# The down projection of a feed-forward block by Strassen's products, with right operands kept in DRAM

## The chip, the cores and the metric

The kernel runs on one core of a Trainium2 chip. The metric is device time in microseconds of one execution; the profile shows one such execution instruction by instruction. All times of the trace are counted from its first instruction.

## The reference, cut to what matters

One decoder block over 1024 tokens of 1024 features, in float32: an mLSTM and a pooling branch, merged by gates, then a gated feed-forward part with 2816 hidden features, and a last norm.

```python
x = x + (g_a * y_a + g_b * y_b) @ w_out[l]
h2 = rms_norm(x, norm2_g[l])
x = x + (silu(h2 @ w_ffn_gate[l]) * (h2 @ w_ffn_up[l])) @ w_ffn_down[l]
return rms_norm(x, final_norm_g)
```

The change is in the product with `w_ffn_down`, (1024 x 2816) @ (2816 x 1024), in what comes before and after it, and in one scratch tile of the mLSTM.

## The kernel before

Tokens lie along the free dimension and features on the 128 partitions, so a tile is 128 features by 1024 tokens, cut into two halves of 512 tokens. There are 8 feature tiles (`KT`) and 22 hidden tiles (`NFF`). Every float32 operand is split into a rounded part and a remainder (`split`, L126 to L128: a cast on ScalarE, a subtraction on VectorE), and `mm3` (L137 to L141) makes a product of two split operands by three matmuls in fp32r.

The stages follow each other: values and gates of the mLSTM, the input projection, the mLSTM itself, the two branches, the output projection, gate/up, down. The input projection and gate/up are done by Strassen's products in Winograd's form (`products`, L209 on): two output tiles at a time, their 8 contraction tiles taken as 4 pairs, in seven products of 4 x 3 matmuls in place of eight. Results are summed from three banks of PSUM, A, B and C, by copies on ScalarE (L219, L221, L223) and sums on VectorE (L225, L227, L229). `pipeline` makes the left operands of job n + 1 ahead of the products of job n. In gate/up a job is one hidden tile: gate and up of that tile are its two outputs. `gated` (L824 on) multiplies by the norm, applies silu (L838 to L841) and stores the hidden tile into `g_d` in DRAM. The right operands of gate/up (`T`, seven kinds by four pairs, x times the norm's gain) stay in SBUF for all 22 jobs.

Down is done without Strassen's products. For the first 512 tokens the loop runs over the hidden tiles outside and the 8 feature tiles inside, with eight banks of PSUM open at once: it loads `w_down[k]` and half of `g_d[k]`, splits both (`first`, `hidden`), and splits the other half of the tile into `gT` for later. Then the norm over these 512 tokens is made and the results are scaled and stored (L908, L909) while the second half runs: feature tile by feature tile, over all 22 hidden tiles, with `w_downc`, the same weights in another order. The last feature tile is done in two pieces of 256 tokens, and the results of the second half are turned by TensorE and stored by rows.

The program is traced by Tile. A planner puts the instructions of each engine in order by its own estimate of the times; where the text has `issue_after`, an instruction is held behind another one of the same engine. Loads and most stores go through the queue of SyncE (SP), in order. Pools reuse memory tile by tile: a tile of a later pool waits for the last reader of the tile that lay there.

In the mLSTM's `attend`, `hf` (two tiles) first takes the squares of the normed numerator (L665, only their sum is used) and then the scaled numerator (L675) that TensorE turns (L677).

Of the kernel before, what the change touches and what calls it, by code (L numbers as in the profile page):

```python
# [8 lines left out]
F32 = mybir.dt.float32  # L9
F32R = mybir.dt.float32r  # L10
# [34 lines left out]
EARLY = 2  # L45
# [18 lines left out]
def tile_hybrid_block(ctx, tc, x, xt, consts, params, w_fm, w_v, w_pool, w_a, w_b, w_out, w_gate, w_up, w_down, w_downc, out, out_rows):  # L64
# [42 lines left out]
    g_d = dram.tile([NFF, P, S], F32, name="g_d")  # L107
# [52 lines left out]
    def operand(dst, src):  # L160
        split(dst[:, 0, :], dst[:, 1, :], src)

    def first_difference(T, kp, lo_k):

        b11, b12 = halves(lo_k)
        nc.vector.tensor_sub(out=b11, in0=b12, in1=b11)
        operand(T["d1"][kp], b11)

    def other_operands(T, kp, lo_k, hi_k, plain=True):

        (b11, b12), (b21, b22) = halves(lo_k), halves(hi_k)
        nc.vector.tensor_sub(out=b11, in0=b22, in1=b11)
        yield operand(T["d2"][kp], b11)
        if plain:
            yield operand(T["b21"][kp], b21)
        nc.vector.tensor_sub(out=b12, in0=b22, in1=b12)
        yield operand(T["d3"][kp], b12)
        if plain:
            yield operand(T["b22"][kp], b22)
        nc.vector.tensor_sub(out=b21, in0=b11, in1=b21)  # L180
        yield operand(T["d4"][kp], b21)
# [167 lines left out]
    with tc.issue_after(stored):  # L349
        for kp in range(KH):  # L350
            first_difference(T, kp, xg[kp])
            list(other_operands(T, kp, xg[kp], xg[kp + KH], False))
# [193 lines left out]
    with ExitStack() as c4:  # L546
# [91 lines left out]
        def attend(h, c, it, state):  # L638
# [3 lines left out]
            nums, hfs = [], []  # L642
            for jj in range(2):
# [20 lines left out]
                hfs.append(t2.tile([P, DH], F32, tag="hf", name="hf"))  # L664
                nc.scalar.activation(out=hfs[jj], in_=num[:, :DH], func=AF.Square, scale=r, accum_out=ss[:, jj:jj + 1])  # L665
# [7 lines left out]
            for jj in range(2):  # L673
                hf = hfs[jj]
# [91 lines left out]
    with ExitStack() as c5:  # L766
# [4 lines left out]
        sq = pool(c9, "sqp", 1, "right").tile([P, S], F32, name="sq")  # L771
        sps = [sp0, None, None]
        ffn = [(w_gate[j], w_up[j]) for j in range(NFF)]
        with ExitStack() as c6:
            xp = pool(c6, "xp", 3, "right")
            pending = None
            for n, j in enumerate(a + b for a in range(KH) for b in (0, KH)):
# [17 lines left out]
                if j < KH:  # L795
                    pending = xs
                    operand(T["b11"][j], halves(xs)[0])
                    first_difference(T, j, xs)
# [4 lines left out]
                list(other_operands(T, j - KH, pending, xs))  # L803
            c3.close()
            sps[1] = pool(c5, "sf1", 6)
# [7 lines left out]
            made = other_operands(T, KH - 1, pending, xs)  # L813
# [6 lines left out]
        ev = pool(c5, "evf", 8)  # L820
        ws.extend(later)
        made_last = split.last

        def gated(j, outs, u1):  # L824
# [8 lines left out]
            for n, (z, u, r) in enumerate(((z2, u2, rsb2[1]), (z1, u1, rsb2[0]))):  # L833
                with ExitStack() as order:
                    if j == NFF - 1 and n >= 0:
                        for made in first.made:
                            order.enter_context(tc.issue_after(made))
# [4 lines left out]
            nc.sync.dma_start(out=g_d[j], in_=outs[0])  # L842
# [14 lines left out]
        dp = pool(c7, "dp", 6, "right")  # L857
        gp = pool(c7, "gp", 6, "right")

        def hidden(pl, k, half):  # L860
            t = pl.tile([P, 2, 512], F32R, tag="g", name="g")
            operand(t, load(g_d[k, :, half * 512:(half + 1) * 512], 512))
            return t

        def first(k):
            w = parts(dp, "d", load(w_down[k]), "wd"), hidden(gp, k, 0)
            if k == 0:
                first.made = split.last
            return w

        ready = [first(k) for k in range(EARLY)]
        last()
    x3p = pool(c7, "x3p", KT, "right")
    sm = pool(c7, "smd", 2, "right")
    gp1 = pool(c7, "gp1", NFF)
    op = pool(c7, "op", 4)

    def residual(j, half, ps):
        r = x3p.tile([P, 512], F32, tag="x3", name="x3")
        with tc.issue_after(load.last.ins):  # L880
            nc.sync.dma_start(out=r, in_=x2_d[j, :, half * 512:(half + 1) * 512])
        nc.vector.tensor_add(out=r, in0=ps, in1=r)
        return r

    def square(r):
        sq = sm.tile([P, 512], F32, tag="sq", name="sq")
        nc.scalar.activation(out=sq, in_=r, func=AF.Square)
        return sq


    ps = [bank("mm" if j < 6 else "aux") for j in range(KT)]
    gT = []
    for k in range(NFF):
        w, g = ready.pop(0) if ready else first(k)
        gT.append(hidden(gp1, k, 1))
        for j in range(KT):
            mm3(ps[j], [a[:, j * P:(j + 1) * P] for a in w], [g[:, a, :] for a in range(2)], k == 0, k == NFF - 1)
    x3 = [residual(j, 0, ps[j]) for j in range(KT)]
    acc = square(x3[0])
    for r in x3[1:]:  # L900
        sq = square(r)
        nc.vector.tensor_add(out=sq, in0=acc, in1=sq)
        acc = sq
    rs = sm.tile([P, 4], F32, tag="rs", name="rs3")
    inverse_rms(sm, token_sums(acc, 4), rs)
    along_rows(sm, rsb2[0], rs, gp.tile([P, 2, 512], F32R, tag="g", name="diag"), 4)
    for j, r in enumerate(x3):
        nc.vector.scalar_tensor_tensor(out=r, in0=r, scalar=col(A_NF, j), in1=rsb2[0], op0=ALU.mult, op1=ALU.mult)  # L908
        nc.sync.dma_start(out=out[j], in_=r)  # L909


    x3 = []
    rows = [op.tile([P, D], F32, tag="o", name="o") for _ in range(4)]
    LAST = KT - 1

# [9 lines left out]
    def feature(j, w, ps, sl, k0, n):  # L925
        for i in range(n):
            k = k0 + i
            mm3(ps, [a[:, i * P:(i + 1) * P] for a in w], [gT[k][:, a, sl] for a in range(2)], k == 0, k == NFF - 1)

    def down_weights(j, k0):  # L930
        n = min(8, NFF - k0)
        return parts(dp, "d", load(w_downc[j, :, k0 * P:(k0 + n) * P], n * P), "wd"), k0, n

    chunks = range(0, NFF, 8)
    for j in range(LAST):
        ps = bank()
        for k0 in chunks:
            w, k0, n = down_weights(j, k0)
            feature(j, w, ps, slice(0, 512), k0, n)
        r = residual(j, 1, ps)  # L940
        sq = square(r)
        nc.scalar.activation(out=r, in_=r, func=AF.Copy, scale=col(A_NF, j))
        x3.append(r)
        if j > 0:
            nc.vector.tensor_add(out=sq, in0=acc, in1=sq)
        acc = sq
        if j == 4:
            for t in range(4):
                turn(t, 0, 4)
    ws = [down_weights(LAST, k0) for k0 in chunks]  # L950
    r = x3p.tile([P, 512], F32, tag="x3", name="x3")
    with tc.issue_after(load.last.ins):
        nc.sync.dma_start(out=r, in_=x2_d[LAST, :, 512:1024])
    x3.append(r)
    sq = sm.tile([P, 512], F32, tag="sq", name="sq")
    ms = sm.tile([P, 4], F32, tag="ms", name="ms")
    rs = sm.tile([P, 4], F32, tag="rs", name="rs3")
    for p in range(2):
# [3 lines left out]
        for w, k0, n in ws:  # L962
            feature(LAST, w, ps, sl, k0, n)
            if p == 0 and k0 == 0:
                for t in range(4):
                    turn(t, 4, LAST)
                nc.vector.tensor_scalar(out=ms, in0=token_sums(acc, 4), scalar1=1.0 / D, scalar2=EPS, op0=ALU.mult, op1=ALU.add)
# [79 lines left out]
```

## Time and profile before

| what | us |
|---|---|
| median of 3 runs (1522.51 to 1526.81) | 1524.85 |
| the profiled execution, whole | 1523.66 |
| its span, first to last instruction | 1521.9 |
| TensorE busy (7237 matmuls) | 1505.1 |
| weight loads busy | 1270.2 |
| VectorE busy | 1018.5 |
| ScalarE busy | 708.9 |

A matmul's end is modelled, and one begins before the one ahead of it has ended, so its work is read from the distance of starts and from the waits, and not from the busy time alone.

### The profile page before, as it was taken

How to read it: one execution, taken by the hardware profiler on the slowest of the kernel's cores; microseconds unless marked ns; L12 is line 12 of the kernel's file. 1: busy time of each engine (PE TensorE's matmuls, PEld its weight loads, DVE VectorE, ACT ScalarE, POOL GpSimd, SP SyncE). 2: the span in 40 equal slices, each digit the busy share in tenths (PEclk: the TensorE clock that was granted, in tenths of full speed). 3: DMA queues.
4: the chain of work that ended last, by engine and by line, in shares of the span. 5: the costliest groups of instructions: out<-in, count | busy, mean ns of one | idle time of the engine just before them, and what ended most of it. 6: DMA issues, size and time to landing. Idle time of an engine off the chain costs nothing.

```text
span 1521.9 us, 19329 instructions
## 1 busy us (share of the span) xinstructions
PE 1505.1 (99%) x7237; PEld 1270.2 (83%) x7237; DVE 1018.5 (67%) x1801; ACT 708.9 (47%) x1256; POOL 27.8 (2%) x58
## 2 busy tenths in 40 slices
PE   9999999999999999999999999999999999999998
PEld 9998888878887799988888788888888888888887
DVE  6767878788867677757567776666666655554432
ACT  6475655566543578752133453333333324443332
POOL 0000000000000011100000000000000000000000
PEclk9999999999999999999999999999999999999999
DMA  6663333323323697718334322222222224664531
GB/s 216 217 230 109 138 120 127 118 105 125 131 84 118 241 324 253 226 57 324 111 131 140 103 83 79 83 83 83 83 83 83 83 77 161 225 220 158 180 107 56
DMA packets 92942, 216.04 MB, mean 142 GB/s; under 512 B 8876, under 2 KB 44844, under 8 KB 92848
## 3 DMA queue, kind: packets, MB, share of 16 engines
q1 hardware_dynamic: 77680, 174.95, 34.6%
q10 hardware_dynamic: 15168, 39.85, 6.9%
q8 instruction: 57, 0.93, 0.3%
q14 instruction: 37, 0.30, 0.1%
HBM read 154.98 MB, written 59.79 MB: 141 GB/s over the span
## 4 chain that ended last, share of the span: by engine, by line
PE 95%; DMA 1%; DVE 1%; ACT 1%; issue 1%; SPq 0%; POOL 0%; POOLq 0%; ACTq 0%; DVEq 0%
PE mm L139 26%; PE mm L141 26%; PE mm L140 26%; PE mm L151 14%; PE aux L141 1%; PE aux L139 1%; PE aux L140 1%; DMA raw<-in_w_a 1%; PE mm L517 0%; PE aux L677 0%; DMA z_d<-o 0%; DMA o<-in_xt 0%; PE aux L566 0%; PE aux L273 0%; DMA rc<-z_d 0%
## 5 line engine op out<-in xcount | busy, mean ns | idle before, releaser
L127 ACT CAST s<-raw 128x512 fp32r<-128x512 f32 x220 | 131.9, 620 | 150.0 <-PE mm L141 106.5
L128 DVE TENSOR_TENSOR s<-raw,s 128x512 fp32r<-128x512 f32 x220 | 147.4, 687 | 36.8 <-ACT s L127 36.3
L139 PE MATMUL mm<-zd,s 128*128 128x512 f32 x352 | 137.5, 393 | 0.3 <-DVE o L227 0.3
L140 PE MATMUL mm<-fd,s 128*128 128x512 f32 x352 | 137.7, 391 | 0.0
L139 PE MATMUL mm<-fd,s 128*128 128x512 f32 x352 | 134.7, 392 | 2.6 <-ACT e L219 2.2
L141 PE MATMUL mm<-fd,s 128*128 128x512 f32 x352 | 137.3, 390 | 0.0
L141 PE MATMUL mm<-zd,s 128*128 128x512 f32 x352 | 137.3, 390 | 0.0
L140 PE MATMUL mm<-zd,s 128*128 128x512 f32 x352 | 137.1, 389 | 0.0
L141 PE MATMUL mm<-g,wdl 128*128 128x512 f32 (+1 forms) x330 | 123.3, 376 | 0.0
L140 PE MATMUL mm<-g,wdh 128*128 128x512 f32 (+1 forms) x330 | 123.1, 375 | 0.0
L139 PE MATMUL mm<-g,wdh 128*128 128x512 f32 (+1 forms) x330 | 120.5, 375 | 0.0
L139 PE MATMUL mm<-zb,s 128*128 128x512 f32 x264 | 103.9, 394 | 0.0
L839 ACT ACTIVATE e<-e 128x512 f32<-128x512 f32 x44 | 27.8, 633 | 162.0 <-DVE e L838 162.0
L128 DVE TENSOR_TENSOR wdl<-raw,wdh 128x1024 fp32r<-128x1024 f32 (+1 forms) x46 | 54.1, 1177 | 73.0 <-ACT wdh L127 73.0
L141 PE MATMUL mm<-fb,s 128*128 128x512 f32 x264 | 102.8, 389 | 0.0
L140 PE MATMUL mm<-zb,s 128*128 128x512 f32 x264 | 102.8, 389 | 0.0
L141 PE MATMUL mm<-zb,s 128*128 128x512 f32 x264 | 102.7, 390 | 0.0
L140 PE MATMUL mm<-fb,s 128*128 128x512 f32 x264 | 102.7, 389 | 0.0
L139 PE MATMUL mm<-fb,s 128*128 128x512 f32 x264 | 99.8, 389 | 0.0
L127 ACT CAST wdh<-raw 128x1024 fp32r<-128x1024 f32 (+1 forms) x46 | 46.7, 1014 | 91.8 <-PE mm L140 54.0
L139 PEld LDWEIGHTS mm<-fd,s 128*128 128x128 f32 x352 | 66.4, 189 | 17.5 <-ACT e L219 2.9
L139 PEld LDWEIGHTS mm<-zd,s 128*128 128x128 f32 x352 | 66.1, 188 | 14.8 <-DVE o L227 0.8
(323 smaller groups left out, 3432.7 us busy)
## 6 DMA issues: line engine op xcount, KB each, us to landing
raw<-in_w_fm SPq DMA_DIRECT2D x44, 512.0 KB, 3.7
z_d<-o ACTq DMA_DIRECT2D x24, 512.0 KB, 2.9
raw<-in_w_gate SPq DMA_DIRECT2D x22, 512.0 KB, 3.7
raw<-in_w_up SPq DMA_DIRECT2D x22, 512.0 KB, 4.2
g_d<-e SPq DMA_DIRECT2D x22, 512.0 KB, 2.6
raw<-in_w_down SPq DMA_DIRECT2D x22, 512.0 KB, 4.3
raw<-g_d SPq DMA_DIRECT2D x44, 256.0 KB, 3.4
q_d<-x ACTq DMA_DIRECT2D x16, 512.0 KB, 2.7
```

The source lines that it names most:

```text
L127: hi_made = nc.scalar.copy(out=hi, in_=src)
L128: split.last = hi_made.ins, nc.vector.tensor_sub(out=lo, in0=src, in1=hi.bitcast(F32)).ins
L139: nc.tensor.matmul(out, lhsT=l[0], rhs=r[0], start=start, stop=False, skip_group_check=resume)
L140: nc.tensor.matmul(out, lhsT=l[0], rhs=r[1], start=False, stop=False, skip_group_check=resume)
L141: mm3.last = nc.tensor.matmul(out, lhsT=l[1], rhs=r[0], start=False, stop=stop, skip_group_check=resume)
L151: nc.tensor.matmul(ps[half], lhsT=l[a], rhs=r[half][b], start=(k == 0 and (a, b) == (0, 0)), stop=(k == nk - 1 and a == 1),)
L839: nc.scalar.activation(out=z, in_=z, func=AF.Silu)
```

## The change

The down projection is done by Strassen's products too, in Winograd's form, for all 1024 tokens at once. The 22 hidden tiles are taken as 11 pairs. The seven right operands of each pair are made as the hidden tiles come out of gate/up: `hidden` splits each into a staging tile (`stage`, three tiles that rotate) and stores it, hi and lo, in `tg_d` in DRAM; of each pair, b11 and d1 are made after the even job, d2, b21 and d3 after the odd one, b22 and d4 after the next even one. `g_d` is gone, and so is one of the two copies of the weights.

The down stage runs over three chunks of 4, 3 and 4 pairs; in a chunk over the seven products (`STEPS`); in a product over the four pairs of feature tiles. The right operands of a step are loaded while the step before runs (13 tiles), left operands are made four products ahead (`EARLY`, 6 tiles), and weights for the next chunk are loaded in the third and the sixth step. After each product VectorE adds the bank to x, which lies in SBUF as 8 tiles for all tokens. In the last chunk the squares are summed as the tiles become final. The two halves of tokens change places: the first 512 are now written by rows at the end, the last 512 by columns.

The pools `sf1` and `evf` have one tile less each, to make room. In the mLSTM the squares go into `rsb`, which is free there, and `hf` is taken only for the scaled values.

```diff
-EARLY = 2
+NPAIR = NFF // 2
+CHUNKS = ((0, 4), (4, 7), (7, 11))
+EARLY = 4
...
-    g_d = dram.tile([NFF, P, S], F32, name="g_d")
+    tg_d = dram.tile([NPAIR, 7, P, S], F32, name="tg_d")
...
-                hfs.append(t2.tile([P, DH], F32, tag="hf", name="hf"))
-                nc.scalar.activation(out=hfs[jj], in_=num[:, :DH], func=AF.Square, scale=r, accum_out=ss[:, jj:jj + 1])
+                nc.scalar.activation(out=rsb[:, jj * DH:(jj + 1) * DH], in_=num[:, :DH], func=AF.Square, scale=r, accum_out=ss[:, jj:jj + 1])
...
-                hf = hfs[jj]
+                hf = t2.tile([P, DH], F32, tag="hf", name="hf")
...
-            sps[1] = pool(c5, "sf1", 6)
+            sps[1] = pool(c5, "sf1", 5)
...
-        ev = pool(c5, "evf", 8)
+        ev = pool(c5, "evf", 7)
+        stp = pool(c5, "stp", 2)
...
+        places = [sqp, stp, stp]
+        def stage(i, b, src):
+            t = places[len(staged) % len(places)].tile([P, 2, 512], F32R, tag="t", name="t")
+            staged.append(t)
+            operand(t, src)
+            nc.sync.dma_start(out=tg_d[i, OPS.index(b)].rearrange("p (a n) -> p a n", a=2), in_=t.bitcast(F32))
+        def hidden(j, z):
+            put = partial(stage, j // 2)
+            if j % 2 == 0:
+                if rest:
+                    list(rest.pop())
+                put("b11", halves(z)[0])
+                first_difference(put, z)
+                even.append(z)
+            else:
+                made = other_operands(put, even.pop(), z)
+                for _ in range(3):
+                    next(made)
+                rest.append(made)
...
-            nc.sync.dma_start(out=g_d[j], in_=outs[0])
+            hidden(j, outs[0])
...
+        s1p = pool(c7, "s1p", KH, "right")
+        rbp = pool(c7, "rbp", KH, "right")
+        tgp = pool(c7, "tgp", 13, "right")
+        ap = pool(c7, "ap", 6, "right")
+        STEPS = ("b21", "d1", "b22", "b11", "d2", "d3", "d4")
+        def down_weights(c, q, fh):
+            k0, k1 = CHUNKS[c]
+            t = (rbp if fh else rawp).tile([P, S], F32, tag="rb" if fh else "raw", name="rb" if fh else "raw")
+            n = (k1 - k0) * P
+            nc.sync.dma_start(out=t[:, :2 * n], in_=w_down[q, fh, :, 2 * k0 * P:2 * k1 * P])
+        def down_lefts(c, q):
...
+            yield op(a12)
...
+            nc.vector.tensor_add(out=s1, in0=a21, in1=a22)
+            t = op(s1)
+            nc.vector.tensor_sub(out=a21, in0=a11, in1=a21)
+            nc.vector.tensor_sub(out=s1, in0=s1, in1=a11)
+            nc.vector.tensor_sub(out=a12, in0=a12, in1=s1)
+            yield t
+            yield op(a12)
+            yield op(a11)
+            yield op(s1)
+            yield op(a21)
+            nc.scalar.activation(out=t[:, 0, :], in_=a22, func=AF.Copy, scale=-1.0)
+            nc.vector.scalar_tensor_tensor(out=t[:, 1, :], in0=a22, scalar=-1.0, in1=t[:, 0, :].bitcast(F32), op0=ALU.mult, op1=ALU.subtract)
+            yield t
+        def down_rights(c, s):
+            for i in range(*CHUNKS[c]):
+                t = tgp.tile([P, 2, 512], F32R, tag="tg", name="tg")
+                nc.sync.dma_start(out=t.bitcast(F32), in_=tg_d[i, OPS.index(STEPS[s])].rearrange("p (a n) -> p a n", a=2))
+        for q in range(KH):
+            down_weights(0, q, 0)
+        down_rights(0, 0)
+        for q in range(KH):
+            down_weights(0, q, 1)
+        for e in range(EARLY):
+            make_ready(e)
         last()
+        list(rest.pop())
...
+    for j in range(KT):
+        t = x3p.tile([P, S], F32, tag="x3", name="x3")
+        nc.sync.dma_start(out=t, in_=x2_d[j])
...
+    def later_tokens():
+        rs = sm.tile([P, 4], F32, tag="rs", name="rs3")
+        inverse_rms(sm, token_sums(acc[1], 4), rs)
+        along_rows(sm, rsb2[0], rs, ap.tile([P, 2, 512], F32R, tag="a", name="diag"), 4)
+        for j in range(KT):
+            r = halves(x3[j])[1]
+            nc.vector.scalar_tensor_tensor(out=r, in0=r, scalar=col(A_NF, j), in1=rsb2[0], op0=ALU.mult, op1=ALU.mult)
+            nc.sync.dma_start(out=out[j], in_=r)
...
+    for e, (c, s, q) in enumerate(entries):
+        final = c == len(CHUNKS) - 1
+        if q == 0:
+            if s + 1 < len(STEPS):
+                down_rights(c, s + 1)
+            elif not final:
+                down_rights(c + 1, 0)
+        make_ready(e + EARLY)
+        if s == 2 and not final:
+            down_weights(c + 1, q, 0)
+        if s == 5 and not final:
+            down_weights(c + 1, q, 1)
+        a, ts = todo.pop(0), rights[c, s]
+        if final and s == 6 and q == KH - 1:
+            break
+        if s == 0:
+            ps = bank()
+        elif s in (1, 2):
+            ps = C[q] = bank() if s == 1 else C[q]
+        else:
+            ps = A[q] = bank() if s == 3 else A[q]
+        product(ps, a, ts, whole, s in (0, 1, 3), True)
+        o = (o10, o21, o11, o10, o11, o21, o20)[s]
+        nc.vector.tensor_add(out=o, in0=ps, in1=o)
...
+        if s == 5:
+            square(q + KH, 1)
+            if q == KH - 1:
+                nc.vector.tensor_add(out=o20, in0=ps, in1=o20)
+                later_tokens()
...
+        product(ps, left, right, sl, True, True)
```

The last product of the last chunk is done in two pieces of 256 tokens, as the last feature tile was before, with the 12 turns of feature tiles 4 to 6 behind the first piece.

## Rows read from the trace of the kernel before

**Rows 1.** The page: span, and busy us of the engines.
```profile
span 1521.9 us, 19329 instructions
...
PE 1505.1 (99%) x7237; PEld 1270.2 (83%) x7237; DVE 1018.5 (67%) x1801; ACT 708.9 (47%) x1256; POOL 27.8 (2%) x58
```

**Rows 2.** The page: the chain that ended last, by engine.
```profile
PE 95%; DMA 1%; DVE 1%; ACT 1%; issue 1%; SPq 0%; POOL 0%; POOLq 0%; ACTq 0%; DVEq 0%
```

**Rows 3.** Stretches: us, busy PE, PEld, DVE, ACT, POOL (instructions); clock, DMA share, GB/s.
```profile
890.00:1250.00 360.00, 360.00 (x1590) 298.09 (x1589) 243.26 (x379) 129.00 (x228) 0.00 (x0) 1.00 0.24 84
260.00:400.00 140.00, 140.00 (x633) 113.53 (x632) 116.76 (x199) 83.75 (x114) 0.00 (x0) 1.00 0.37 128
...
1267.00:1387.00 120.00, 120.00 (x532) 99.34 (x531) 63.11 (x78) 50.25 (x68) 0.00 (x0) 1.00 0.68 226
1387.00:1514.00 127.00, 126.70 (x647) 108.26 (x645) 48.91 (x67) 40.75 (x60) 1.71 (x2) 1.00 0.34 107
```

**Rows 4.** TensorE's waits over the whole run: us in total, times, longest.
```profile
PE mm L139 <- ACT e L219: 2.2, 1, 2.2
...
PE mm L151 <- ACT ya L127: 0.5, 1, 0.5
...
PE mm L139 <- DVE e L227: 0.4, 1, 0.4
```

**Rows 5.** Groups by form, TensorE, 1260 to 1522: busy us, mean ns, idle before.
```profile
L139 PE MATMUL mm<-g,wdh 128*128 128x512 f32 x286 | 107.9, 389 | 0.0
...
L139 PE MATMUL aux<-g,wdh 128*128 128x512 f32 x44 | 16.5, 389 | 0.0
...
L139 PE MATMUL mm<-g,wdh 128*128 128x256 f32 x44 | 12.5, 285 | 0.0
```

**Rows 6.** Timeline, full matmuls of the down stage: start us, us, instruction.
```profile
1359.79 0.39 PE L139 MATMUL mm<-g,wdh 128*128 128x512 f32 x1
...
1370.67 0.39 PE L139 MATMUL mm<-g,wdh 128*128 128x512 f32 x1
```

**Rows 7.** Timeline, half matmuls of the last feature tile.
```profile
1509.47 0.28 PE L141 MATMUL mm<-g,wdl 128*128 128x256 f32 x1
...
1513.43 0.28 PE L141 MATMUL mm<-g,wdl 128*128 128x256 f32 x1
```

**Rows 8.** Timeline, VectorE in gate/up; in brackets the idle time before.
```profile
1119.60 0.69 DVE L202 TENSOR_TENSOR raw<-raw 128x512 f32<-128x512 f32 x1
1120.20 0.68 DVE L841 TENSOR_TENSOR e<-mm,e 128x512 f32<-128x512 f32 x1
...
1127.50 0.69 DVE L840 TENSOR_TENSOR e<-e,rsb 128x512 f32<-128x512 f32 x1 [0.70 <-ACT e L839]
...
1139.24 0.68 DVE L841 TENSOR_TENSOR e<-mm,e 128x512 f32<-128x512 f32 x1
```

**Rows 9.** Groups: ScalarE's cast (whole run), VectorE's half (890 to 1250).
```profile
L127 ACT CAST s<-raw 128x512 fp32r<-128x512 f32 x220 | 131.9, 620 | 150.0 <-PE mm L141 106.5 <-DVE raw L197 29.9 <-PE mm L151 4.8
...
L128 DVE TENSOR_TENSOR s<-raw,s 128x512 fp32r<-128x512 f32 x91 | 59.8, 689 | 19.4 <-ACT s L127 19.4
```

**Rows 10.** DMA issues: KB each, median us from issue to landing.
```profile
g_d<-e SPq DMA_DIRECT2D x22, 512.0 KB, 2.6
```

**Rows 11.** Stretches with the busiest DMA on rows of 4 KB.
```profile
690.00:700.00 10.00, 10.00 (x46) 8.29 (x45) 9.35 (x13) 2.84 (x5) 0.00 (x0) 1.00 0.98 379
700.00:710.00 10.00, 10.00 (x46) 8.29 (x45) 8.22 (x12) 2.74 (x4) 0.00 (x0) 1.00 0.98 338
```

**Rows 12.** Timeline, VectorE, the norm of the first 512 tokens.
```profile
1406.11 0.16 DVE L253 TENSOR_SCALAR ms<-aux 128x4 f32<-128x4 f32 x1 [2.31 <-PE aux L273]
...
1416.22 5.38 DVE L908 SCALAR_TENSOR_TENSOR x<-x,par,rsb 128x512 f32<-128x512 f32 x8
```

**Rows 13.** The stretch around TensorE's wait at the entry of gate/up.
```profile
850.00:855.00 5.00, 2.76 (x9) 1.91 (x8) 4.84 (x8) 2.20 (x5) 0.00 (x0) 0.82 0.28 82
```

**Rows 14.** ScalarE's waits in the mLSTM, 540 to 690.
```profile
ACT hf L665 <- PE aux L677: 6.3, 3, 4.4
```

More of the change, by code (lines that the diff above doesn't have):

```diff
@@ L856, in tile_hybrid_block @@
         c7 = ctx.enter_context(ExitStack())
[L857 to L869, printed above, removed]
@@ L872, in tile_hybrid_block @@
+        early_made = []
+        for q in range(KH):
[5 more added lines that the diff above has]
+            make_ready(e)
+            if e == 1:
+                early_made.extend(split.last)
         last()
-    x3p = pool(c7, "x3p", KT, "right")
-    sm = pool(c7, "smd", 2, "right")
-    gp1 = pool(c7, "gp1", NFF)
+        list(rest.pop())
+    x3p = pool(c7, "x3p", KT)
     op = pool(c7, "op", 4)
[L878 to L909, printed above, removed]
+    sm = pool(c7, "smd", 2)
@@ L916, in turn, with scaled @@
+    def scaled(j):
+        r = halves(x3[j])[0]
+        nc.scalar.activation(out=r, in_=r, func=AF.Copy, scale=col(A_NF, j))
     def turn(t, j0, j1):
@@ L923, in turn @@
         copy(out=rows[t][:, j0 * P:j1 * P], in_=ps[:, :n])
[L925 to L949, printed above, removed]
@@ new lines, in product @@
+    def product(ps, a, ts, sl, start, stop):
+        for kp, t in enumerate(ts):
+            mm3(ps, [a[:, i, kp * P:(kp + 1) * P] for i in range(2)], [t[:, i, sl] for i in range(2)], start and kp == 0, stop and kp == len(ts) - 1, True)
+    A, C = [None] * KH, [None] * KH
+    whole = slice(0, 512)
+    for e, (c, s, q) in enumerate(entries):
[11 more added lines that the diff above has]
+        a, ts = todo.pop(0), rights[c, s]
+        (o10, o11), (o20, o21) = halves(x3[q]), halves(x3[q + KH])
+        if final and s == 6 and q == KH - 1:
+            break
+        if s == 0:
+            ps = bank()
[6 more added lines that the diff above has]
+        nc.vector.tensor_add(out=o, in0=ps, in1=o)
+        if not final:
+            continue
+        if s == 3:
+            square(q, 0)
+            scaled(q)
+        if s == 4:
+            square(q, 1)
+            if q == 1:
+                for t in range(4):
+                    turn(t, 0, KH)
+        if s == 5:
[3 more added lines that the diff above has]
+                later_tokens()
+        if s == 6:
+            square(q + KH, 0)
+            scaled(q + KH)
@@ L956, in tile_hybrid_block @@
+    r, left, right = o20, a, ts
+    sq = sqd.tile([P, 512], F32, tag="sq1", name="sq")
     ms = sm.tile([P, 4], F32, tag="ms", name="ms")
@@ L961, in tile_hybrid_block @@
         ps = bank()[:, :256]
[L962 to L967, printed above, removed]
+        product(ps, left, right, sl, True, True)
+        if p == 0:
+            for t in range(4):
+                turn(t, KH, LAST)
+            nc.vector.tensor_scalar(out=ms, in0=token_sums(acc[0], 4), scalar1=1.0 / D, scalar2=EPS, op0=ALU.mult, op1=ALU.add)
         nc.vector.tensor_add(out=r[:, sl], in0=ps, in1=r[:, sl])
```

85 lines of the change are left out of this document (57 added, 28 removed).

## The prediction

> **What bounds the kernel now.** I read four views in this order: busy time of the engines, the chain that ended last, TensorE's own waits, and busy time by stage. TensorE is busy for 1505.1 of 1521.9 us [rows 1] and has 95% of the chain that ended last [rows 2]. Busy time alone would not prove that it works without holes, since a matmul is shown as 0.39 us and the next one starts before it ends. So I took the distance of starts in the stage that is rewritten: L139 at 1359.79 and L139 at 1370.67 are 48 matmuls apart, 10.88/48 = 0.2267 us each [rows 6], and in the last feature tile 33 matmuls of 256 columns lie between 1509.47 and 1513.43, 0.120 us each [rows 7]. The groups by form give 286 + 44 matmuls of 512 columns for each of L139 to L141 and 44 of 256 [rows 5], that is 990 full and 132 half ones: 990 x 0.2267 + 132 x 0.120 = 240.3 us. The stage runs from 1267 to 1514, 247 us [rows 3]; transposes and token sums fill the rest. The products of gate/up and down wait only twice, 2.2 us at the entry of gate/up and 0.4 us at its exit [rows 4]. So the stage lasts as long as its matmuls, and VectorE (112 of 247 us in its two parts together) and the DMA (226 and 107 GB/s) have room there [rows 3]. The gate/up stage before it is as full: 360.00 of 360 us [rows 3].
>
> **The matmuls removed.** Seven products for each of 4 pairs of feature tiles, over 11 pairs of hidden tiles, three matmuls each: 7 x 4 x 11 x 3 = 924 in place of 528 + 528. The last product of the last chunk (12 of them) is done as 24 halves. So 912 full and 24 half ones are left: 78 full and 108 half ones go, 78 x 0.2267 + 108 x 0.120 = 17.7 + 13.0 = **-30.6 us**. Transposes (28 + 4), token sums and the broadcast of the norm are the same in number. The Trainium skill's page "TensorE: Matmul & The Clock Gate", section "Back-to-back issue gap", gives 518 and 262 cycles at 2.4 GHz, 216 and 109 ns, so by it the saving would be an estimated 28.6 us; the rows show 226.7 and 120 ns for these fp32r matmuls at a granted clock of 1.00, and the rows decide.
>
> **Operands moved into gate/up.** The 44 splits of hidden tiles leave the down stage (`hidden`, L860) and 77 staged operands (11 pairs x 7) come into gate/up: 3.5 splits (a ScalarE cast, a VectorE subtraction), 2 more subtractions and 3.5 stores of 512 KB per job in place of one store. A job's period is 1139.24 - 1120.20 = 19.04 us, and VectorE instructions of this size that follow each other (1119.60, 1120.20) start 0.60 us apart [rows 8]. VectorE has 243.26/18.9 = 12.9 us of work per job now [rows 3]; 5.5 x 0.60 = 3.3 more make 16.2, 85% of the period. ScalarE goes from 129.00/18.9 = 6.8 to 6.8 + 3.5 x 0.62 = 9.0 us, 47% [rows 3, 9]. The input projection shows what such a load does: the same `products`, VectorE at 116.76 of 140 us (83%) and ScalarE at 60%, TensorE at 140.00 of 140 [rows 3]. So I cost it at nothing, with the products of the same job as its cover, and put +0.5 us for the first and last jobs. If the cover is gone, it shows up in one place: product d3 needs the copy of A, and d4 the sum at L227, each with one other product (12 x 0.2267 = 2.7 us) in between. Three staging tiles rotate, so a fourth cast in a row waits for the first one's store, 2.6 us from issue to landing [rows 10]. Behind that cast stand the PSUM copies L219 to L223 on ScalarE, and TensorE behind them; the wait would be about 1 us, inside the 2.7. On SP's queue a staged store waits for its VectorE half, and the weight loads of the next job stand behind it; they are used a job later. The pools that shrink (sf1 6 to 5, evf 8 to 7) leave two jobs of operands and the six tiles that four jobs hold at once, so I see no wait there. Bounds: 0 to the second rival's price.
>
> **The start of the down stage.** New tiles lie where the gate/up operands lay. The first (`rbp`) is free when the last job's first product ends, 16.3 us before that job's end, and the second step of products begins 10.9 us after it: 27.2 us. In them the DMA has to bring four weight halves, two steps of four right operands, and half to all of the eight residual tiles (traced ahead of the second step), and to store some four staged operands: 20 to 24 tiles of 0.524 MB, 10.5 to 12.6 MB. The busiest rows of this trace with 4 KB rows move 379 and 338 GB/s at a share of 0.98 [rows 11]. At 379 this takes 27.7 to 33.2 us, at 338 31 to 37: the second step would be 0.5 to 10 us late, or not at all if the residuals come earlier or later than that. I take **+3**, nearer the low end, since half of the residual tiles can be loaded a job earlier. The Trainium skill's page "DMA: Bandwidth & Descriptors", section "Where 436 GB/s comes from", puts the ceiling at 435 GB/s; by it the estimate would be 24 to 29 us, no more than 2 late. No row here comes near it over 10 us, so I stay with the rows. A stall of this kind can cost more than its length: in the 5 us around the one 2.2 us wait the mean granted clock is 0.82, so part of them ran at the level of 1.2 GHz [rows 4, 13].
>
> **Inside the down stage.** Each product (2.7 us, 2.0 in the middle chunk) brings on VectorE one sum from PSUM, half a split and 4/7 of an addition: about 1.55 us of 2.7, 57%; in the last chunk the squares' sums make it 78%. ScalarE has a cast of 0.62 us. Left operands are made four products ahead, a sum has three products until its bank is used again: **+0.5**. The DMA must bring 24 right operands, the residuals and 3.1 MB of weights in chunk one, 21.5 MB with the first of chunk two in 76 us, 283 GB/s; under both rows of 338 and 379, with a step or two of prefetch.
>
> **The end.** Before, the last half tile's 66 matmuls (7.9 us) cover the first half's norm, and the other 512 tokens were scaled a good 90 us earlier [rows 12]. Now both token halves end together. From the last matmul's start at 1513.43 the end comes 8.5 us later [rows 1, 7]; that chain stays. What is added: only 12 half matmuls (1.4 us) cover the first half's scaling, and the other tokens' norm (before: 10.1 us from its mean at 1406.11 to the first scaling at 1416.22, then eight in 5.38 us [rows 12]) falls into the last four products, 11 us. Its eight scalings and eight stores then stand on VectorE and SP ahead of or among the final sums. Bounds 0 (all fits) to +5.4 (all eight in front); I take **+2.5**.
>
> **mLSTM.** `hf` had two tiles for the squares and the scaled values, so a square waited for the transposes of the chunk before: 6.3 us in three times on ScalarE [rows 14]. Writing the squares into `rsb` removes that; the last reader of the old `rsb` there is the deferred sigmoid, which is over before the first square. TensorE waited 0.5 us for the last `ya` at the entry of the next stage [rows 4], which the longest of the three (4.4 us) may have made late. I take **-0.5**, between 0 and -1.5.
>
> **Sum.** -30.6 + 0.5 + 3 + 0.5 + 2.5 - 0.5 = -24.6 us. The profiled execution took 1523.66 us, 1.8 more than its span and 1.2 less than the median of 1524.85. On its own scale that gives 1499.1, on that of the median 1500.2: I say **1500**. With all bounds at their good ends it is 1492, with all bad ones (start +10, end +5.4) 1510.
>
> **Rivals.**
> *The DMA sets the down stage.* The stage now moves 40.4 MB of right operands, 11.5 of weights, 4.2 of residuals and no longer reads `g_d`: 56 MB. At the 226 GB/s that the stage showed before [rows 3] this takes 248 us, and the whole gain is gone: about 1525; at 250 GB/s 224 us, 1511. It decides from 264 GB/s (56 MB in 212 us) down. Against it: that 226 was at a share of 0.68, and 338 to 379 are shown [rows 11]. Chance 0.12, 1510 to 1525.
> *VectorE becomes the bound of gate/up* (the other side). If its 26.5 instructions per job cost the 0.69 us of one that stands alone, and the waits for ScalarE stay (0.70 us in front of L840 twice a job [rows 8], and 19.4/18.9 = 1.0 us before the splits, 1.5 with 10.5 of them in place of 7 [rows 9]), a job takes 18.3 + 1.4 + 1.5 = 21.2 us, 2.2 over its 19.04; over 21 jobs +46 us, 1545. It eats the gain from 20.2 us per job on. For it: an 11th of VectorE's time is left only if its gaps can be filled, in order. Against it: the input projection at 83%. Chance 0.09, 1522 to 1545.
> *The gain is not had because TensorE is not the bound* would need holes that the starts do not show; it gets no share of its own.
>
> **Chances.** The forecast 0.79 (1491 to 1511). The range 1491 to 1515 takes in the first quarter of the DMA rival and leaves out about 2 in 10. This kernel's runs lie within 0.3% of each other, so 4.6 us is what a measurement can tell. Faster: 0.79 + 0.08 of the DMA rival = 0.87; same: 0.04 + 0.02 of VectorE's low end = 0.06; slower 0.07.
>
> **What will show it.** Right: 912 full and 24 half matmuls, 0.2267 us apart; VectorE near 85% in gate/up with no TensorE wait for L219 or L227; a hole of at most a few us about 11 us into the down stage that a `tg` or `x3` load ends; last matmul to end 9 to 14 us. Wrong: TensorE's waits in every gate/up job (second rival), or `tg` loads ending its waits step after step with the DMA share near 1 (first).

## The result, and the profile after

The changed kernel takes 1509.01 us in the median of four runs (1508.38 to 1509.98), beside 1524.5 for four runs of the kernel before: the ratio is 0.9894, 95% interval 0.988 to 0.9908. It is faster by 15.5 us, where the sum of the prediction had 24.6. Direction and bound were right, the time was inside the range, and 9 us of the forecast gain are missing.

The page of the changed kernel, to be read beside [rows 1, 2]:

```profile
span 1508.3 us, 19546 instructions
...
PE 1480.2 (98%) x7051; PEld 1249.0 (83%) x7051; DVE 1130.9 (75%) x2033; ACT 729.3 (48%) x1327; POOL 28.5 (2%) x58
...
PE 95%; DVE 2%; DMA 1%; issue 1%; ACT 0%; SPq 0%; POOLq 0%; POOL 0%; ACTq 0%; DVEq 0%
```

TensorE still has 95% of the chain, with 186 matmuls less (7237 - 7051 = 78 + 108). But between its busy time and the span there are now 28.1 us, where there were 16.8. TensorE's longest waits after the change, in total, times, longest, beside [rows 4]:

```profile
PE mm L143 <- ACT a L131: 7.4, 1, 7.4
PE aux L280 <- DVE ms L1073: 5.5, 1, 5.5
PE mm L143 <- ACT e L226: 2.2, 1, 2.2
...
PE mm L143 <- DVE e L234: 0.8, 1, 0.8
```

Two new holes, 7.4 and 5.5 us long, each a single event. The other two were there before, with 2.2 and 0.4 us. By groups of one form, 1260 to 1509, the products are those that were counted, 3 x 304 full and 3 x 8 half ones:

```profile
L143 PE MATMUL mm<-tg,a 128*128 128x512 f32 x304 | 119.9, 395 | 7.4 <-ACT a L131 7.4
...
L143 PE MATMUL mm<-tg,a 128*128 128x256 f32 x8 | 2.3, 292 | 0.0
```

Two matmuls of the new stage that are 48 apart:

```profile
1359.22 0.39 PE L145 MATMUL mm<-tg,a 128*128 128x512 f32 x1
...
1370.10 0.39 PE L145 MATMUL mm<-tg,a 128*128 128x512 f32 x1
```

(1370.10 - 1359.22)/48 = 0.2267 us, the distance of [rows 6]. By stretches (columns as in [rows 3]): gate/up, the start of the down stage in four pieces, its rest, and the end:

```profile
890.00:1250.00 360.00, 360.00 (x1590) 298.22 (x1589) 309.75 (x492) 167.44 (x298) 0.00 (x0) 1.00 0.44 158
...
1262.00:1278.00 16.00, 15.22 (x68) 12.28 (x67) 14.01 (x24) 4.10 (x7) 0.00 (x0) 1.00 0.98 376
1278.00:1286.00 8.00, 0.56 (x4) 0.16 (x2) 8.00 (x15) 1.99 (x4) 0.00 (x0) 0.72 1.03 399
1286.00:1291.00 5.00, 5.00 (x12) 3.94 (x13) 3.42 (x6) 0.18 (x1) 0.00 (x0) 0.50 1.00 397
1300.00:1320.00 20.00, 20.00 (x89) 16.54 (x89) 12.46 (x20) 5.37 (x9) 0.00 (x0) 1.00 1.01 405
1320.00:1490.00 170.00, 170.00 (x774) 141.50 (x773) 111.28 (x183) 53.24 (x94) 1.01 (x1) 1.00 0.54 196
1494.00:1508.00 14.00, 1.70 (x6) 1.21 (x6) 7.37 (x16) 2.97 (x7) 1.39 (x2) 0.59 0.81 300
```

Gate/up stays full with VectorE at 86%, and the down stage is full from 1300 on. What is lost lies between 1278 and 1291 and behind the last product. SP's queue at the first place (start, us, issues; one landing time is told below):

```profile
1245.47 13.08 SPq L838 DMA_DIRECT2D tg_d<-t  x3
1258.65 4.84 SPq L938 DMA_DIRECT2D tg<-tg_d  x4
1263.55 4.71 SPq L900 DMA_DIRECT2D rb<-in_w_down  x4
1268.31 6.33 SPq L970 DMA_DIRECT2D x<-x_d  x8
1275.60 2.88 SPq L938 DMA_DIRECT2D tg<-tg_d  x3
```

The second step's first right operand is issued at 1275.60, behind sixteen tiles of 512 KB, and lands at 1285.81; TensorE's last matmul of the first step is at 1278.11 and its next one at 1285.94:

```profile
1278.11 0.39 PE L145 MATMUL mm<-tg,a 128*128 128x512 f32 x1
1285.94 0.77 PE L143 MATMUL mm<-tg,a 128*128 128x512 f32 x1 [7.44 <-ACT a L131]
1286.51 0.63 PE L144 MATMUL mm<-tg,a 128*128 128x512 f32 x1
1286.93 0.63 PE L145 MATMUL mm<-tg,a 128*128 128x512 f32 x1
...
1291.63 0.42 PE L144 MATMUL mm<-tg,a 128*128 128x512 f32 x1
```

The bracket names a cast of ScalarE. The cast that ended just then, at 1285.94, makes an operand for a later step (`a<-raw`); the first left operand of the second step (`a<-s`: cast at 1273.22, subtraction at 1275.52) was whole at 1276.2. The load that landed 0.13 us before the matmul fits. Behind the hole the starts are 0.427 us apart: the granted clock is 0.50, the level of 1.2 GHz, for another 5 us, and 13 distances cost 5.69 - 13 x 0.2267 = 2.7 us more.

At the end, VectorE and then SP's queue:

```profile
1493.71 5.38 DVE L1004 SCALAR_TENSOR_TENSOR x<-x,par,rsb 128x512 f32<-128x512 f32 x8
1499.01 0.15 DVE L1073 SCALAR_TENSOR_TENSOR ms<-aux,ms 128x2 f32<-128x2 f32 x1
```
```profile
1494.48 4.97 SPq L1005 DMA_DIRECT2D out<-x  x8
1500.48 4.45 SPq L1089 DMA_DIRECT2D out<-o  x8
```

The eight scalings of the later tokens stand in front of the last row norm, which TensorE needs (the wait of 5.5 us), and their eight stores in front of the last eight. The last product's matmul starts at 1490.99, the end is 17.3 us later; before it was 8.5.

The two profiled executions, cut at three marks:

| from .. to | before | after | difference |
|---|---|---|---|
| begin .. first product of the input projection | 96.0 | 100.05 | +4.0 |
| .. first product of gate/up | 733.8 | 730.0 | -3.8 |
| .. start of the last product matmul | 683.6 | 660.9 | -22.7 |
| .. end | 8.5 | 17.3 | +8.8 |

The first line isn't the change's: its code there is the same, and in the kernels below, all the same up to that mark, it comes between 95.6 and 100.1.

### The profile page after: what moved, and what is told of

It is laid out like the page before. It is cut to its first block, busy times and chain, and to the rows that moved or that the text cites. A ratio compares the mean times of both kernels' runs of the same rounds, so it can differ in the third digit from the quotient of the medians.

```text
span 1508.3 us, 19546 instructions
## 1 busy us (share of the span) xinstructions
PE 1480.2 (98%) x7051; PEld 1249.0 (83%) x7051; DVE 1130.9 (75%) x2033; ACT 729.3 (48%) x1327; POOL 28.5 (2%) x58
## 4 chain that ended last, share of the span: by engine, by line
PE 95%; DVE 2%; DMA 1%; issue 1%; ACT 0%; SPq 0%; POOLq 0%; POOL 0%; ACTq 0%; DVEq 0%
PE mm L143 26%; PE mm L145 26%; PE mm L144 26%; PE mm L155 14%; DMA v<-v_d 1%; PE aux L683 0%; PE mm L524 0%; DMA yb<-yb_d 0%; DVE x L1004 0%; PE aux L573 0%; DMA o<-in_xt 0%; DVE a L132 0%; PE aux L280 0%; PE mm L993 0%; PE aux L143 0%
## 5 line engine op out<-in xcount | busy, mean ns | idle before, releaser
L143 PE MATMUL mm<-tg,a 128*128 128x512 f32 (+1 forms) x312 | 122.3, 392 | 7.4 <-ACT a L131 7.4
L144 PE MATMUL mm<-tg,a 128*128 128x512 f32 (+1 forms) x312 | 121.7, 390 | 0.0
L145 PE MATMUL mm<-tg,a 128*128 128x512 f32 (+1 forms) x312 | 121.6, 390 | 0.0
L1037 DVE TENSOR_TENSOR x<-mm,x 128x512 f32<-128x512 f32 x83 | 57.2, 689 | 63.0 <-PE mm L145 62.9
L143 PE MATMUL mm<-fb,s 128*128 128x512 f32 x264 | 103.0, 391 | 0.0
L144 PE MATMUL mm<-fb,s 128*128 128x512 f32 x264 | 103.0, 390 | 0.0
L145 PE MATMUL mm<-fb,s 128*128 128x512 f32 x264 | 102.7, 390 | 0.0
L143 PEld LDWEIGHTS mm<-fd,s 128*128 128x128 f32 x352 | 66.3, 188 | 17.8 <-ACT e L226 2.9
L143 PEld LDWEIGHTS mm<-zd,s 128*128 128x128 f32 x352 | 66.1, 188 | 14.7 <-DVE o L234 0.8
L145 PEld LDWEIGHTS mm<-fd,s 128*128 128x128 f32 x352 | 66.4, 189 | 13.9
L144 PEld LDWEIGHTS mm<-zd,s 128*128 128x128 f32 x352 | 66.1, 188 | 14.1 <-issue 0.5
```

Of the source, the lines that this page charges most:

```text
L143: nc.tensor.matmul(out, lhsT=l[0], rhs=r[0], start=start, stop=False, skip_group_check=resume)
L144: nc.tensor.matmul(out, lhsT=l[0], rhs=r[1], start=False, stop=False, skip_group_check=resume)
L145: mm3.last = nc.tensor.matmul(out, lhsT=l[1], rhs=r[0], start=False, stop=stop, skip_group_check=resume)
L1037: nc.vector.tensor_add(out=o, in0=ps, in1=o)
```

## The experiments

Ten kernels. All but one start from the changed kernel (the mLSTM one from the kernel before); only the edits shown differ. Times are medians, and ratios are against runs of the kernel before on the same chip (1525.86, 1525.61 and 1526.02 us in three sets of runs).

**The order of the loads.** In the first, the second step's right operands are requested ahead of the residual tiles; in the second the residuals also come in halves, each before the step that adds to it.

```diff
+    down_rights(0, 1)
     for j in range(KT):
         t = x3p.tile([P, S], F32, tag="x3", name="x3")
...
-            if s + 1 < len(STEPS):
+            if (c, s) == (0, 0):
+                pass
+            elif s + 1 < len(STEPS):
```

> Edit: the right operands of the second step are requested ahead of the eight residual tiles, nothing else. Theory A (bytes in front: at some 395 GB/s each tile of 0.524 MB ahead in the queue is 1.3 us): the hole of 7.5 us in front of the second step goes, but 16 loads must still be through before the third step, so 3 to 6 us of it come back there; 1503 to 1507 us. Theory B (the loads only start late, since SP stands at staged stores until 1258): the same order of loads starts at the same time, total as A. Theory C (the left operands are late, since VectorE works without a gap from 1264 to 1289): the hole stays where it is, 1509 us.

```diff
+    def residual(s):
+        j0, half = {0: (0, 0), 1: (KH, 1), 2: (0, 1), 6: (KH, 0)}[s]
+        for j in range(j0, j0 + KH):
+            nc.sync.dma_start(out=halves(x3[j])[half], in_=x2_d[j, :, half * 512:(half + 1) * 512])
+    residual(0)
+    down_rights(0, 1)
+    residual(1)
...
+            if (c, s) == (0, 0):
+                down_rights(0, 2)
+                residual(2)
...
+                if (c, s) == (0, 4):
+                    residual(6)
```

> Edit: the residual is loaded in halves in the order in which the steps add to it, the last quarter only in the fifth step. Theory A: two tiles fewer (1.05 MB, 2.7 us) stand in front of the third step than with the whole tiles; the holes add up to 1 to 4 us, 1499 to 1503 us. Theory C: no change, 1509 us.

Measured 1502.98 us (0.9853, 0.9836 to 0.9869) and 1501.23 (0.984, 0.9826 to 0.9855). In the first the hole shrinks to 2.0 us, now for a sum on VectorE, and 1.0 for a load. VectorE has no gap there and comes to that sum at 1284.21, though the first residual tile had landed at 1279.85:

```profile
PE mm L143 <- DVE x L1040: 2.0, 1, 2.0
...
PE mm L143 <- DMA tg<-tg_d: 1.0, 1, 1.0
```

In the second no wait there is longer than 0.8 us, and the stretch keeps the full clock.:

```profile
1262.00:1300.00 38.00, 35.62 (x152) 27.90 (x152) 32.74 (x55) 10.72 (x18) 0.00 (x0) 1.00 1.01 385
```

The DMA is as busy as before and TensorE has no long stop: it was the order of the bytes and not their sum. The small holes that are left between 1240 and 1310 add up to 3.8 us, where the changed kernel has 11.4 (distances of starts beyond 0.2267). Left operands and VectorE's work are the same in both, so they were not the cause of the long hole.

**The queue of the staged stores.** SP's row of 13.08 us above looked like a queue that is stuck behind staged stores. Here they are issued from ScalarE's queue.

```diff
-            nc.sync.dma_start(out=tg_d[i, OPS.index(b)].rearrange("p (a n) -> p a n", a=2), in_=t.bitcast(F32))
+            nc.scalar.dma_start(out=tg_d[i, OPS.index(b)].rearrange("p (a n) -> p a n", a=2), in_=t.bitcast(F32))
```

> Edit: the staged operands are stored through ScalarE's queue in place of SP's. Theory B: the first loads of the down stage start some 8 us earlier (about 1250 in place of 1258.65), the hole in front of the second step shrinks to 0 to 2 us, 1499 to 1502 us. Theory A alone (the memory they load into is not free earlier): they start where they did, 1507 to 1510 us. In gate/up ScalarE now also issues 3.5 stores per job, 0.33 us each; it has half its time free, no TensorE wait there by either.

Measured 1509.01 us (0.989, 0.9875 to 0.9905), no gain. One load of the first step left earlier, at 1248.81; the other three at 1259.01, 1259.39 and 1262.41, within 1 us of where they were. The wait is still there, now under its true name:

```profile
1248.81 13.92 SPq L938 DMA_DIRECT2D tg<-tg_d  x4
```
```profile
PE mm L143 <- DMA tg<-tg_d: 8.8, 1, 8.8
```

So it isn't the queue's head alone that keeps the loads until 1259. What SP waits for in this kernel between 1247 and 1266 us:

```profile
SPq L938 <- PE mm L145: 22.9, 3, 10.7
```

Three of the four loads wait for matmuls of gate/up (until 1248.8, 1259.0 and 1262.4), the last readers of the memory that they go into. No run here frees it earlier.

**The order at the end.** The later tokens' eight scalings and stores (`later_scaled`, the loop of `later_tokens`) are held behind the last row scaling.

```diff
-                        nc.vector.tensor_scalar_mul(out=o, in0=src, scalar1=rs[:, t:t + 1])
+                        made = nc.vector.tensor_scalar_mul(out=o, in0=src, scalar1=rs[:, t:t + 1])
...
+    with tc.issue_after(made.ins):
+        later_scaled(0, KT)
```

> Edit: the eight scalings of the later tokens (and so their stores) are issued behind the last scaling of the rows. If VectorE's order sets the end: the wait of 5.5 us for L1073 goes, the rows end near 1498 and the eight scalings with their stores near 1505; the end 2 to 4 us sooner, 1505 to 1507 us. If the 4.2 MB of stores at the end set it: within 1 us of 1509.

Measured 1508.65 us (0.9887, 0.9872 to 0.9902). The 5.5 us wait for L1073 is gone, and the time isn't: from the last product to the end it is 17.5 us. SP's queue is one row of stores:

```profile
1494.05 4.47 SPq L1091 DMA_DIRECT2D out<-o  x8
1498.61 5.40 SPq L1007 DMA_DIRECT2D out<-x  x8
```

**Without those stores.** The same order; seven of the eight column stores of tokens 512 to 1023 are left out, so most of that half of the output isn't written.

```diff
-            nc.sync.dma_start(out=out[j], in_=r)
+            if j == 0:
+                nc.sync.dma_start(out=out[j], in_=r)
...
```

> The order of e4 with seven of the eight 256 KB column stores of the later 512 tokens left out (only the first column is stored, so most of tokens 512 to 1023 isn't written). In e4 sixteen stores left one after another between 1494.05 and 1504 us, 0.60 to 0.69 us apart. If these stores set the end (theory: the end was mis-sized because the last 4.2 MB go out in one line), seven of them at 0.66 us are 4.6 us, and with what they hold up the end comes 4 to 6 us sooner than e4: 1502.5 to 1504.5 us. Rival: the chain square, row sum, scaling and the last store's own landing set the end whatever else is in the queue: within 1.5 us of e4, 1507 to 1510 us.

Measured 1503.06 us (0.9851, 0.9837 to 0.9864), 5.6 below the one with all stores; from the last product to the end 12.6 us in place of 17.5. The stores did set the end.

**Two queues.** The order of the kernel with all stores, every second one of the sixteen from ScalarE's queue.

```diff
-                nc.sync.dma_start(out=out_rows[t * P:(t + 1) * P, c0:c1], in_=rows[t][:, c0:c1])
+                (nc.scalar if t % 2 else nc.sync).dma_start(out=out_rows[t * P:(t + 1) * P, c0:c1], in_=rows[t][:, c0:c1])
...
-            nc.sync.dma_start(out=out[j], in_=r)
+            (nc.scalar if j % 2 else nc.sync).dma_start(out=out[j], in_=r)
...
```

> The order of e4, with every second one of the sixteen 256 KB stores at the end issued from ScalarE's queue in place of SP's. In e4 they leave 0.60 to 0.69 us apart, and 256 KB in 0.66 us are 397 GB/s, about what the stage at 1262 to 1320 us moved with its DMA share at 1.0 (393 to 405 GB/s). If the bytes set the spacing (theory), two queues give nothing: 1506.5 to 1509.5 us beside e4's 1508.7, and the stores land no closer together. Rival: one queue's own issuing sets it; then eight stores a queue are out in half the time, some 4 us sooner: 1503.5 to 1505.5 us.

Measured 1509.54 us (0.9892, 0.9879 to 0.9906). The column stores, SP's queue and then ScalarE's:

```profile
1495.69 4.97 SPq L1007 DMA_DIRECT2D out<-x  x4
```
```profile
1496.88 4.99 ACTq L1007 DMA_DIRECT2D out<-x  x4
```

Four issues now take what eight took; the last traced landing is at 1504.89, and in the kernel with one queue at 1505.70. It is the data and not the issuing: 256 KB each 0.66 us are 397 GB/s. The Trainium skill's page "Perfetto Trace Analysis", section "Optimizing DMA Performance", reads a queue that is solid with DMA slices as one bound by the making of descriptors; here the queue was solid, a second one gave nothing, and the measurement decides.

**The mLSTM's squares alone**, in the kernel before.

```diff
-            nums, hfs = [], []
+            nums = []
...
-                nc.scalar.activation(out=hfs[jj], in_=num[:, :DH], func=AF.Square, scale=r, accum_out=ss[:, jj:jj + 1])
+                nc.scalar.activation(out=rsb[:, jj * DH:(jj + 1) * DH], in_=num[:, :DH], func=AF.Square, scale=r, accum_out=ss[:, jj:jj + 1])
...
-                hf = hfs[jj]
+                hf = t2.tile([P, DH], F32, tag="hf", name="hf")
```

> The kernel before with one part of the change alone: the squares of the mLSTM written to the tile that is free there, in place of a tile of the ring that the later steps need. The prediction gave it 0.5 us (0 to 1.5): 1524.0 us beside 1524.5. The trace of the changed kernel shows TensorE's holes between 540 and 687 us at 3.0 us where the kernel before has 6.7: if that is this edit's doing, 3.6 us, 1520.5 to 1521.5 us. If the holes closed for another reason (addresses, chance), no change: 1523.5 to 1525.5 us.

Measured 1522.63 us in 11 runs beside 1525.61 in 15 (0.9981, 0.9972 to 0.999): 3.0 us, 1.5 to 4.3. The totals that were expected, reckoned from 1524.5, were all missed; the gain is near the 3.6 us read from the trace. TensorE's waits between 540 and 690 us in the kernel before, and then with the edit alone:

```profile
PE mm L139 <- ACT kt L570: 1.1, 1, 1.1
PE mm L139 <- ACT cs L127: 1.0, 1, 1.0
PE mm L151 <- ACT ya L127: 0.5, 1, 0.5
...
PE mm L140 <- DVE cs L128: 0.3, 1, 0.3
PE mm L141 <- DVE pl L128: 0.2, 1, 0.2
```
```profile
PE mm L151 <- ACT wah L127: 0.9, 1, 0.9
PE aux L676 <- ACT hf L674: 0.4, 1, 0.4
```

Four waits for operands that ScalarE and VectorE make (`kt`, `cs`, `pl`) are gone, together 2.6 us. They were not waits for a square that was held up: ScalarE's squares stood for 6.3 us in three times [rows 14], which ended at 589.0, 598.0 and 675.0 us, and TensorE's waits for `kt` and `cs` of ScalarE ended at 608.2 and 660.0. With the edit ScalarE still waits for those transposes, now at the scaled values:

```profile
ACT hf L674 <- PE aux L676: 4.9, 2, 3.8
```

The order on ScalarE changed too: before, a square (start 658.84) stands ahead of that `cs` (659.35); with the edit `cs` (656.03) comes ahead of the squares. That the gain is the edit's is shown; that it comes by this order is not.

**VectorE nearer its limit.** Four more subtractions per gate/up job, on data that nobody reads again.

```diff
                     nc.vector.tensor_mul(out=z, in0=u, in1=z)
+            for _ in range(4):
+                nc.vector.tensor_sub(out=u2, in0=u2, in1=u2)
```

> The changed kernel with four more VectorE subtractions of 128x512 at the end of each of the 22 gate and up jobs, on data that nobody reads again. VectorE is at 86% of that stretch now (16.3 us of a 19.0 us period); four times about 0.6 us make 18.7, 98%. If only the sum of VectorE's work counts, TensorE still doesn't wait for it: 1507 to 1511 us. Rival (the prediction's second one, a VectorE that bounds the stage by its order): TensorE starts to wait for L219 or L227 operands in each job; with 0.5 us a job that is 11 us, 1515 to 1525 us.

Measured 1509.08 us (0.9889, 0.9876 to 0.9903).

```profile
890.00:1250.00 360.00, 360.00 (x1590) 298.10 (x1589) 347.18 (x572) 164.27 (x296) 0.00 (x0) 1.00 0.44 158
```
```profile
PE mm L143 <- DMA tg<-tg_d: 10.9, 1, 10.9
```

At 96% (98 was expected) TensorE waits for VectorE not once in this stage. VectorE comes out of it later: the first load of the down stage is issued 5.8 us before the last job's end, in place of 8.8, and the wait at its start is 10.9 us in place of 7.4. All holes there add up to 12.8 us in place of 11.4, and the median is the same within 0.1 us.

**Both losses mended.** Loads by need, and in the last chunk the products in the order d1, b22, b11, d2, d3, b21, d4, so that the later tokens are done two steps before the end.

```diff
+        FINAL = (1, 2, 3, 4, 5, 0, 6)
+        def step(c, s):
+            return FINAL[s] if c == len(CHUNKS) - 1 else s
...
```

> Loads by need as in e2, and in the last chunk of the down projection the seven products in another order, so that both column blocks of the later 512 tokens are complete two products before the end; their scalings and their stores (2.1 MB) then go out under the last two products, some 22 us. If the two holes are all that kept the change from its sum, the end falls from 17.3 us behind the last product's start back to some 9 to 10 (8.5 in the kernel before): 6 to 8 us below e2's 1501.2, that is 1493 to 1496 us. Rival: the new order takes the PSUM banks in which the next product wants to start, or asks for left operands earlier than they are made, and TensorE waits in the last chunk what it gains at the end: 1500 us or more, with a TensorE wait of several us between 1400 and 1490 us in the trace.

Measured 1499.5 us (0.9827, 0.9813 to 0.984), under both kernels and 1.7 below loads by need alone, not 6 to 8; the intervals of these two overlap. From the last product to the end it is 12.3 us (17.3 there), but from the first product of the stage to the last one 219.8 (215.8 there). Of these 4.0 us, 2.2 are waits of TensorE for copies that stand behind the scalings on VectorE:

```profile
PE mm L1009 <- DVE o L1011: 2.2, 2, 2.0
```
```profile
1475.09 5.39 DVE L1020 SCALAR_TENSOR_TENSOR x<-x,par,rsb 128x512 f32<-128x512 f32 x8 [0.38 <-ACT rsb L274]
1480.40 0.68 DVE L997 TENSOR_TENSOR sq<-sq 128x512 f32<-128x512 f32 x1
1481.00 1.28 DVE L1011 COPY o<-mm 128x512 f32<-128x512 f32 x2
```

The last attempt puts one product behind the matmuls that spread the norms, and takes these copies to ScalarE.

```diff
-        copy = nc.scalar.copy if t % 2 else nc.vector.tensor_copy
+        copy = nc.scalar.copy if t % 2 or j0 == 0 else nc.vector.tensor_copy
...
+            if summed and (s, q) == (0, 2):
+                order.enter_context(tc.issue_after(summed[0].ins))
...
```

> e6 with two orders changed behind its trace, in which the eight scalings of the later tokens started at 1475.1 us (the row of their reciprocal norms came 4.3 us after its operand was ready, since the second of its two matmuls stood behind products) and then held up two copies for which TensorE waited 2.2 us. Here the third of the four products of that step stands behind those two matmuls, and the first copies of turned blocks are all on ScalarE, which was idle there for 5.5 us. If VectorE's burst of scalings is what e6 lost, TensorE's 2.8 us of waits there go and the stores go out 4 us sooner: 1495.5 to 1498 us beside e6's 1499.5. Rival: the end is set by the last eight row stores (2.1 MB, 4.5 us) and the work right in front of them, and TensorE waits for the row of norms instead: within 1 us of e6, 1498.5 to 1500.5.

Measured 1500.14 us (0.9828, 0.9814 to 0.9841): the rival, within 1 us. The scalings start 3.3 us sooner and the end takes 11.0 us, but TensorE stood in front of the norms, and at the lower clock behind them:

```profile
PE aux L273 <- ACT diag L272: 2.9, 1, 2.9
```
```profile
1462.00:1469.00 7.00, 4.07 (x13) 3.03 (x13) 3.48 (x7) 5.55 (x14) 1.01 (x1) 0.77 0.01 2
```

## Why the prediction was right in kind and off in size

The saving by the matmuls removed and the places of the losses were right, three sizes were not. That the time still fell into the range is in part luck: the start of the down stage and the end both came out beyond their bad bounds (10.8 over 10, 6.5 over 5.4), and the mLSTM, beyond its good one, gave 3 us back.

*The matmuls removed, -30.6.* Right: the counts and the distance of 0.2267 us are those of the trace. The -22.7 of the table is this, +10.8 for the holes below, -0.5 at the entry of gate/up, and -2.3 for matmuls that aren't products (row sums, turns, rows of norms): by the distance of their starts they take 16.1 us up to that mark, 18.4 before, and the rest now stands behind it.

*Operands moved into gate/up, +0.5.* Measured 0: 360.00 of 360 us busy, VectorE at 86% where 85% was computed. The rival of a bound by VectorE fell further with the extra subtractions: even at 96% its order leaves no wait inside the stage. Its price was also reckoned too high: 379 instructions in 18.9 jobs [rows 3] and 5.5 more are 25.6 a job and not 26.5 (after: 492 in 18.9, 26.0).

*The start of the down stage, +3.* This is the larger failed step. The hole is where it was expected, 10.7 us into the stage, and a load ends it; its size was wrong. Summed as distance of starts beyond 0.2267, the holes between 1240 and 1310 went from 0.7 to 11.4 us: **+10.8**, 7.6 of it the hole and 2.7 the half clock. The prediction had a window of 27.2 us for the loads, from the end of the last job's first product, 16.3 us before that job's end. The job ends at 1267.5, so this was 1251.2; the loads began at 1258.65, 7.5 us later. SP stood at a staged store until then, and waited for matmuls of that job before its loads at 1259.78, 1263.17 and, the second of `rbp`, 1266.97: the memory came free bit by bit until the job's end. And "half of the residual tiles can be loaded a job earlier" was wrong: all eight, 4.2 MB, were issued from 1268.31 on, ahead of the second step's operands; at 393 to 399 GB/s they are 10.5 to 10.7 us of transfer. Two assumptions about when loads may start, each with no row behind it, stand behind the +3. The second weighs more: loads by need, with the same late start, leave 3.8 of the 11.4 us.

The rate was the lesser question: the rows after show 376 to 405 GB/s where 338 to 379 was used. The Trainium skill's page "DMA: Bandwidth & Descriptors", section "Where 436 GB/s comes from", has 435 GB/s as the fabric's ceiling, by which the prediction's estimate was at most 2 us late, and about 358 as the limit for transfers between HBM and SBUF. The stretches here with a full share lie between the two, none above 405. The lateness came from the order and not the rate. That a hole costs more than its length was said, but not put into the sum.

*The rival of a down stage set by the DMA.* It fell: 20 us at a share of 1.01 with TensorE at 20.00 of 20, then 196 GB/s for the rest. The DMA is near its full share for some 60 us (1262 to 1320) and not for 220.

*Inside the down stage, +0.5.* Measured 0 from 1300 on.

*The end, +2.5.* The second failed step. It grew by 8.8 us, 2.3 of them the matmuls that moved there, so **+6.5**, more than the bound of +5.4. The place was named ("eight scalings and eight stores ... ahead of or among the final sums"), but only the scalings were priced. The stores cost as much: sixteen of 256 KB in one line are 10.5 us at 0.66, where the kernel before had eight left. Two limits of nearly the same length lay over each other, so taking away the scalings alone gave nothing, and the stores set the time once they were behind.

*mLSTM, -0.5.* Mis-sized: -3.0 by the runs of the edit alone, -3.8 between the first two marks of the table (-3.5 with the edit alone), and more than its own bound of -1.5. The prediction followed one wait of TensorE (for `ya`, 0.5 us). The waits that went with the edit are four others, for `kt`, `cs` and `pl`, and the square's own wait, which the prediction named as the reason, for the most part only moved on to the scaled values (6.3 us before, 4.9 after). Why those four went stays open.

*Sum.* -30.6 + 0 - 0.5 + 10.8 + 0 + 6.5 - 3.8 = -17.6; with the +4.0 of the begin it is the -13.6 of the two spans. The medians give -15.5. Since the begin alone varies by more than 4 us, the 2 us between are not told apart here.

## What to carry to other kernels

Where a stage begins in memory that the stage before frees, write the line of loads down in order, with sizes and the time from which each may start, and compare each landing with its first reader: what is needed first goes first, and a load cut in halves can go by need. At a kernel's end count the bytes of the stores as well as the work in front of them; if two limits are of one length, mending one shows nothing. And a small edit that rides along should be run alone: this one was worth six times what the one wait in mind let expect, by a way that this wait did not show.

## What the runs showed of the hardware that was not expected

- One core's DMA moved 385 to 405 GB/s at a share of 1.00 to 1.03 with tiles of 512 KB, loads and stores mixed, for 20 us (405) and 38 us (385, with loads by need) at a time.
- A hole of 7.4 us in front of TensorE was followed by 5 us at a granted clock of 0.50, and one of 2.9 us by some six distances of 0.427 us.
- The trace put the 7.4 us down to a cast for a later product that ended in the same moment; in the kernels with edits that left this hole alone the same wait is named as the load.
- The time to the first product of the input projection varied from 95.6 to 100.1 us over executions of the same code, more than many an edit here is worth.
